# Short-convolution layer on one core: f's deep operand prepared later, and V' read ahead of d's split

## The chip, the cores and the metric

The kernel runs on one core of a Trainium2 chip. The metric is device time in microseconds (us). The kernel before takes 794.39 us, the median of three runs (793.05 to 795.4). Its engines are named as in the profile: PE (TensorE's matmuls; PEld its weight loads), DVE (VectorE), ACT (ScalarE), POOL (GpSimd) and SP (SyncE, which only issues transfers).

## The reference

One layer of a hybrid encoder; with the depth used here it is the short-convolution mixer in a sandwich norm. x is 1024 positions by 1024 channels in float32, and each branch is 2048 wide.

```python
def short_conv_mixer(u, w_in, conv_w, w_out):
    z, bg, cg, v = jnp.split(u @ w_in.astype(u.dtype), 4, axis=-1)
    y = bg * causal_dwconv(cg * v, conv_w) * jax.nn.silu(z)
    return y @ w_out.astype(u.dtype)

h = h + rms_norm(short_conv_mixer(rms_norm(h, pre), ...), post)
```

The input projection is 1024 x 1024 by 1024 x 8192, the convolution has three taps along the positions, and the output projection is 1024 x 2048 by 2048 x 1024.

## The kernel before, in words

**Precision.** Every operand of a matmul is split into a high part in fp32r and a low part, the rest. A product is done in three passes: low by high, high by low, high by high (L221 to L223, 128x128 by 128x512; L780 to L782, 128x128 by 128x256, in the smaller products). A split is an ACT instruction for the high part (a CAST) and a DVE subtraction for the low part. `split` (L160, L161), `split_high` and `split_low` (L168, L187) let DVE read the source from SBUF. `split_by_bank` (L181 to L183) has ACT copy the source into a PSUM bank, named beside, as well, and DVE reads it there; there is one such bank.

**Products.** The channels are worked in chunks c = p // 2 of two pairs p each: the even pair holds the columns CG and V, the odd pair Z and BG. The four block products of a pair are done as seven, a to g, with sums and differences of weight blocks (`add_s` on POOL, L148 to L156) and of the operand u (the tiles u_a to u_g, made once). A product of a pair is twelve 512-wide matmuls: wal, wah and so on are the low and high parts of its weight operand in the current pair, and px and pv are its banks in PSUM. From chunk DEEP = 3 on product b, and from chunk DEEP_F = 4 on product f, are replaced, for the two pairs of a chunk at once, by seven products of half the size. These are the slots written "bX'" and "fX'" below ("fc" is f's product c'); six 256-wide matmuls each, with weight operands dwb and dwf and the sums dsb and dsf behind them (`deep_sums`, L734 to L738, POOL).

**f's operand.** Product f of a chunk in seven needs u_f in another form. It is made once, in three steps:

- `deep_parts("f", [k])`: high and low part of quarter k of u_f are added on POOL into a page deepf (L701, 128x512). Four of them.
- `deep_subs("f", [k])`: four differences on POOL (L707 to L710, 128x256) on the quarters k and k + 2. Two calls, eight instructions.
- `deep_split("f", i)` for i = c', e', d', g': two halves each, ACT writes the high part ufXh (L160), DVE the low part ufXl (L161).

The same three steps make the operand of product b before, in pairs 4 to 6.

**Order.** PE's order is the list `slots`, built by hand. A tile framework gives each engine its instructions in the order in which the Python loop issues them, and each engine runs its queue in that order. After the matmuls of a slot the loop calls `prepare(n)`, which issues the splits of weights for all slots that start within LEAD = 7.0 us of the end of this one by a fixed clock (2.72 us for a product, 0.72 for a small one). Then comes the slot's own follow-up: `after(p, i)` (copies of a bank to SBUF on ACT, L229; additions and products on DVE and POOL), `deep_after` for b's small products (L787), `deep_after_f` for f's (L803 to L816). Then come transfers, weight sums, pieces of the output side, and last the entry of the table `UNDER`, if there is one for this slot. `UNDER` is what places the steps of the operands of b and f.

Around the change a chunk with f in seven goes like this on PE. Even pair: c, e, b a', b b', d, f a', f b', a of the next pair, b c', b e', g. Odd pair: c, f c', f e', e, b f', f f', b d', f d', d, b g', f g', a of the next pair, g. So the bank X' (px2f, from f c') and the bank V' (pv2f, from f e') are both finished around product e, and `deep_after_f` adds each to a half of the page snc on DVE (L814, 128x256). f f', later, adds onto V's bank again, so PE has to wait until L814 has read it.

In pairs 6 to 8, where f's operand is made, the last chunk without f in seven (c = 3) also ends with its convolution: gate (L271), first tap on ACT (L657), two more on DVE (L666), then the products with the gates and SiLU (L248 to L258, L1012, L1017), and the output y.

Of the kernel before, what the change touches and what calls it, by code (L numbers as in the profile page):

```python
# [17 lines left out]
DEEP_F = 4  # L18
# [5 lines left out]
def kernel(  # L24
# [48 lines left out]
    def page(name, dtype=F32, shape=(HB,)):  # L73

        return pages.tile([P, *shape], dtype, tag="pg", name=name, bufs=PAGES)
# [83 lines left out]
    def split(src, hi, lo):  # L159
        nc.scalar.copy(hi, src)  # L160
        nc.vector.tensor_sub(lo, src, hi.bitcast(F32))  # L161
# [8 lines left out]
    def by_seven(z, c):  # L170

        return c >= DEEP if z == "b" else DEEP_F <= c < NC - 1
# [524 lines left out]
    def deep_parts(z, ks):  # L697

        for k in ks:
            deep[z, k] = page(f"deep{z}{k}")  # L700
            nc.gpsimd.tensor_add(deep[z, k], UH[z][:, k].bitcast(F32), UL[z][:, k].bitcast(F32))  # L701

    def deep_subs(z, ks):

        for k in ks:
            (b11, b12), (b21, b22) = ((t[:, :HH], t[:, HH:]) for t in (deep[z, k], deep[z, k + KQ]))
            nc.gpsimd.tensor_sub(b12, b12, b11)  # L707
            nc.gpsimd.tensor_sub(b22, b22, b12)
            nc.gpsimd.tensor_sub(b11, b22, b11)
            nc.gpsimd.tensor_sub(b21, b21, b22)  # L710
# [3 lines left out]
    def deep_split(z, i):  # L714

        k0, l0 = DEEP_U[i]
        ls = slice(l0, l0 + HH)
        own = z == "f" or i != "e'"
        if own:
            deep[z, i] = [tmp.tile([P, KQ, HH], F32R, tag="ub", name=f"u{z}{i[0]}{h}_deep", bufs=14) for h in "hl"]  # L720
        for k in range(KQ):
            hi, lo = (t[:, k] for t in deep[z, i]) if own else (UH[z][:, k, ls], UL[z][:, k, ls])
            split(deep[z, k0 + k][:, ls], hi, lo)
# [212 lines left out]
    for p in range(2, len(PAIRS)):  # L936
# [29 lines left out]
        ("a", 2 * DEEP): lambda: (deep_split("b", "c'"), deep_split("b", "e'")),  # L966
        ("g", 2 * DEEP - 1): lambda: deep_split("b", "d'"),
        ("c", 2 * DEEP): lambda: deep_split("b", "g'"),
        ("d", 2 * DEEP_F - 3): lambda: deep_parts("f", [0]),
        ("f", 2 * DEEP_F - 3): lambda: deep_parts("f", [2]),  # L970
        ("d", 2 * DEEP_F - 2): lambda: deep_parts("f", [1]),
        ("f", 2 * DEEP_F - 2): lambda: deep_parts("f", [3]),
        ("g", 2 * DEEP_F - 2): lambda: deep_subs("f", [0]),
        ("c", 2 * DEEP_F - 1): lambda: deep_subs("f", [1]),
        ("e", 2 * DEEP_F - 1): lambda: deep_split("f", "c'"),
        ("d", 2 * DEEP_F - 1): lambda: deep_split("f", "e'"),
        ("f", 2 * DEEP_F - 1): lambda: deep_split("f", "d'"),
        ("g", 2 * DEEP_F - 1): lambda: deep_split("f", "g'"),
    }


# [7 lines left out]
    def prepare(n):  # L989
        while ready[0] < len(slots) and at[ready[0]] < at[n + 1] + LEAD:  # L990
            slot = slots[ready[0]]
            if slot[2:]:
                z, i, c = slot
                deep_prep(z, c, i)
            elif slot[::-1] not in wt:
                split_w(*slot[::-1])
            ready[0] += 1

    first_chunk("")
    for n, slot in enumerate(slots):  # L1000
        if slot[2:]:
            z, i, c = slot
            deep_product(z, c, i)
            prepare(n)
            if z == "f":
                deep_after_f(c, i)
                continue
            deep_after(c, i)
            if (i, c) == ("f'", NC - 1):
                third_unit(0)  # L1010
            elif i == "g'" and not by_seven("f", c):
                nc.scalar.activation(sn[2 * c + 1, "a"], sn[2 * c + 1, "a"], AF.Silu)  # L1012
            continue
        i, p = slot
        f7 = by_seven("f", p // 2)
        product(p, i)
        prepare(n)  # L1017
        after(p, i)
        q, prev = p + 1, p // 2 - 1
        if p == 2:  # L1020
            first_chunk(i)
        if i == "c":
            if p % 2 and p // 2 < DEEP:
                nc.scalar.activation(sn[p, "a"], sn[p, "a"], AF.Silu)
            if p % 2 == 0 and p in TODO:
                fetch_t(TODO[q])
            if p % 2 == 0 and p > 2:
                fetch_s(prev)
            if p % 2 == 0 and p in TODO:
                add_t(TODO[p], [0, 1])  # L1030
            if p % 2 == 0 and p // 2 >= DEEP:
                deep_sums("b", p // 2, 1)
        elif i == "e":
            add_s(q, "ecdf" if f7 else "ec")
            if f7 and p % 2 == 0:
                for part in (0, 1):
                    deep_sums("f", p // 2, part)
            if p % 2 and q in TODO:
                fetch_t(TODO[q])
            elif p in TODO and p % 2 == 0:  # L1040
                add_t(TODO[p], [2, 3])
        elif i == "d":
            if p + 2 <= END:
                fetch(p + 2)
            if not f7:
                add_s(q, "d")
            if p in TODO and p % 2 == 0:
                add_t(TODO[q], [0, 1])
            if p % 2 == 0 and p > 2:
                add_y(prev)  # L1050
        elif i == "f":
            add_s(q, "f")
            if p == 2:
                add_y(0)
        elif i == "g":
            if p % 2 and q <= END and q // 2 >= DEEP:
                deep_sums("b", q // 2, 0)
        elif i == "a":
            if prev >= 0 and p % 2 == 0 and by_seven("f", prev):
                for t in (sn[p - 1, "c"], sn[p - 1, "a"]):  # L1060
                    nc.scalar.activation(t, t, AF.Silu)
                nc.gpsimd.tensor_mul(cvs[prev][:, HB:], sn[p - 1, "c"], sn[p - 1, "e"])
            if p % 2 and p in TODO:
                add_t(TODO[p], [2, 3])
        if DEEP < NC and (i, p) in UNDER:
            UNDER[i, p]()
        if p == END - 1 and i in "cd":
            fetch_unit()
        if p == END:
            if i in "acg":  # L1070
                split_unit()
            elif i == "d":
                third_unit(2)
            if i in "ac":
                fetch_unit()
            elif i == "d":
                load_small("b", "B2")
            elif i == "f":
                load_small("b", "A1")
                load_small("b", "B1")  # L1080
                fetch_s(NC - 1)
            elif i == "g":
                for n in ("A2", "B3", "X"):
                    load_small("b", n)
                split_small("b", "B2")
                split_small("b", "B1")
                sums_y("b", "d", nc.vector)
                split_small("b", "A1")
# [238 lines left out]
```

## Time and profile before

| | before |
|---|---|
| median of three runs | 794.39 us |
| profiled execution | 794.88 us |
| its span | 793.1 us |
| PE busy | 773.6 us |
| DVE busy | 649.9 us |
| ACT busy | 420.1 us |
| POOL busy | 392.4 us |
| mean granted clock of TensorE | 0.993 |

The span is the time from the first to the last instruction that the profile shows; the profiled execution's own time is 1.8 us longer. A line of the timeline gives the start in us, the busy time in us, the engine, the source line, the operation, output<-inputs, the tile's shape, and how many instructions the line stands for. In brackets stands the idle time just before it, and the instruction whose end let it go. Matmuls overlap: a 512-wide one shows 0.39 us, but the next starts 0.23 us after it.

### The profile page before, as it was taken

The page shows a single profiled execution, that of the slowest core. Times are in us where ns is not written, and L with a number is a line of the kernel's source. Part 1 is how long each engine was busy: PE and PEld are TensorE (multiplying, and loading weights), DVE is VectorE, ACT ScalarE, POOL GpSimd, SP SyncE. Part 2 cuts the span into 40 slices and gives each one's busy share as a digit, 9 for nine tenths or more (in the row PEclk, how much of TensorE's full clock was granted, in tenths as well). Part 3 has the DMA queues.
Part 4 walks back from the last instruction along what each step waited for, and adds up shares of the span by engine and source line. Part 5 has one row for each costly group of instructions (what it writes and reads, how often), then busy time and mean ns, then how long its engine had stood idle before and what let it go on. Part 6 is the DMA issues. An engine that isn't in the chain of part 4 may idle for free. (4 is left out here: it accounts for less than half of the span.)

```text
span 793.1 us, 11970 instructions
## 1 busy us (share of the span) xinstructions
PE 773.6 (98%) x4050; PEld 664.7 (84%) x4050; DVE 649.9 (82%) x964; ACT 420.1 (53%) x775; POOL 392.4 (49%) x337
## 2 busy tenths in 40 slices
PE   8999999896999999999999999999999999999996
PEld 7888888785888888888888888888888889889985
DVE  6899657977587888888979798876779899986985
ACT  7655424335455556465554646464644565844821
POOL 2516579667364737384747474746555110630041
PEclk9999999998999999999999999999999999999999
DMA  9211431312327364453748383725243979885445
GB/s 318 55 54 31 116 108 38 94 53 79 119 95 219 120 193 155 158 185 127 239 127 259 107 271 110 256 82 158 74 127 107 346 250 351 306 260 190 130 159 186
DMA packets 115822, 127.18 MB, mean 160 GB/s; under 512 B 7416, under 2 KB 74032, under 8 KB 115760
## 3 DMA queue, kind: packets, MB, share of 16 engines
q1 hardware_dynamic: 115744, 126.41, 49.4%
q8 instruction: 32, 0.52, 0.3%
q14 instruction: 30, 0.25, 0.1%
q10 hardware_dynamic: 16, 0.00, 0.0%
HBM read 91.78 MB, written 34.60 MB: 159 GB/s over the span
## 5 line engine op out<-in xcount | busy, mean ns | idle before, releaser
L252 POOL TENSOR_TENSOR sne<-sne,cv 128x512 f32<-128x512 f32 x15 | 20.7, 1378 | 154.7 <-DVE cv L666 126.1
L182 ACT COPY beside<-raw 128x512 f32<-128x512 f32 x77 | 45.5, 590 | 31.6 <-DVE dwb1l L183 21.5
L221 PE MATMUL px<-u_c,wcl 128*128 128x512 f32 x124 | 49.2, 397 | 7.1 <-ACT sna L229 7.1
L229 ACT COPY sna<-px 128x512 f32<-128x512 f32 x30 | 17.6, 587 | 66.1 <-PE px L223 66.1
L152 POOL TENSOR_TENSOR se<-raw,raw 128x512 f32<-128x512 f32 x31 | 49.3, 1589 | 5.6 <-DMA raw<-in_sc_w_in 4.1
L666 DVE SCALAR_TENSOR_TENSOR cv<-gpad,cw,cv 128x1024 f32<-128x1024 f32 x32 | 42.2, 1319 | 11.4 <-ACT cv L657 11.2
L223 PE MATMUL px<-u_c,wch 128*128 128x512 f32 x124 | 49.0, 395 | 0.0
L222 PE MATMUL px<-u_c,wch 128*128 128x512 f32 x124 | 49.0, 395 | 0.0
L221 PE MATMUL px<-u_d,wdl 128*128 128x512 f32 x124 | 48.6, 392 | 0.0
L221 PE MATMUL px<-u_a,wal 128*128 128x512 f32 x124 | 48.6, 392 | 0.0
L222 PE MATMUL px<-u_a,wah 128*128 128x512 f32 x124 | 48.5, 391 | 0.0
L222 PE MATMUL px<-u_d,wdh 128*128 128x512 f32 x124 | 48.5, 391 | 0.0
L222 PE MATMUL px<-u_g,wgh 128*128 128x512 f32 x124 | 48.4, 391 | 0.0
L221 PE MATMUL px<-u_g,wgl 128*128 128x512 f32 x124 | 48.4, 390 | 0.0
L222 PE MATMUL pv<-u_e,weh 128*128 128x512 f32 x124 | 48.4, 390 | 0.0
L221 PE MATMUL pv<-u_e,wel 128*128 128x512 f32 x124 | 48.4, 390 | 0.0
L223 PE MATMUL px<-u_d,wdh 128*128 128x512 f32 x124 | 48.4, 390 | 0.0
L223 PE MATMUL px<-u_a,wah 128*128 128x512 f32 x124 | 48.3, 389 | 0.0
L223 PE MATMUL px<-u_g,wgh 128*128 128x512 f32 x124 | 48.3, 389 | 0.0
L223 PE MATMUL pv<-u_e,weh 128*128 128x512 f32 x124 | 48.2, 389 | 0.0
L154 POOL TENSOR_TENSOR sc<-se,raw 128x512 f32<-128x512 f32 x31 | 46.0, 1485 | 2.4
L148 POOL TENSOR_TENSOR raw<-raw,raw 128x512 f32<-128x512 f32 x31 | 46.2, 1491 | 0.0
(538 smaller groups left out, 2739.8 us busy)
## 6 DMA issues: line engine op xcount, KB each, us to landing
raw<-in_sc_w_in SPq DMA_DIRECT2D x128, 256.0 KB, 4.3
y_d<-cv SPq DMA_DIRECT2D x16, 512.0 KB, 3.3
s_d<-s SPq DMA_DIRECT2D x32, 256.0 KB, 3.5
t<-in_sc_w_out SPq DMA_DIRECT2D x32, 256.0 KB, 3.7
t_d<-t SPq DMA_DIRECT2D x32, 256.0 KB, 4.0
tb<-in_sc_w_out SPq DMA_DIRECT2D x16, 256.0 KB, 4.3
s<-y_d SPq DMA_DIRECT2D x16, 256.0 KB, 4.9
xr<-in_x SPq DMA_DIRECT2D x16, 256.0 KB, 3.8
```

Source lines behind the costliest of these rows:

```text
L148: nc.gpsimd.tensor_sub(t, block(p, 0, 0), t)
L152: nc.gpsimd.tensor_add(t, block(p, 1, 0), block(p, 1, 1))
L154: nc.gpsimd.tensor_sub(t, sums[p, "e"], block(p, 0, 0))
L182: nc.scalar.copy(b, src)
L221: nc.tensor.matmul(ps, lo, UH[i][:, k], start=first and k == 0, stop=False, skip_group_check=True)
L222: nc.tensor.matmul(ps, hi, UL[i][:, k], start=False, stop=False, skip_group_check=True)
L223: nc.tensor.matmul(ps, hi, UH[i][:, k], start=False, stop=last, skip_group_check=True)
L229: nc.scalar.copy(t, banks[p, "v" if i == "e" else "x"])
L252: nc.gpsimd.tensor_mul(t, t, cvs[c][:, HB:])
L666: nc.vector.scalar_tensor_tensor(cvs[c], gpad[:, j : j + L], tap(c, j), cvs[c], op0=ALU.mult, op1=ALU.add)
```

## The change

f's operand is prepared later. Its four sums (L701) stood behind d5, f5, d6 and f6; now two stand behind d6, one behind f6, one behind g6. Its differences stood behind g6 and c7; now behind e7 and d7. Its splits stood behind e7, d7, f7 and g7, in the last chunk with f whole; now behind c8, e8, d8 and a9, in the first chunk with f in seven, each ahead of the small product that reads it. The first small products that read them are f c', f e', f d' and f g' of chunk 4.

The loop also changes where it handles f c' and f e': the two reads L814 are issued before `prepare`, and after f c' `prepare` is left out, so that what it would have issued comes after f e'.

```diff
-        ("d", 2 * DEEP_F - 3): lambda: deep_parts("f", [0]),
-        ("f", 2 * DEEP_F - 3): lambda: deep_parts("f", [2]),
-        ("d", 2 * DEEP_F - 2): lambda: deep_parts("f", [1]),
-        ("f", 2 * DEEP_F - 2): lambda: deep_parts("f", [3]),
-        ("g", 2 * DEEP_F - 2): lambda: deep_subs("f", [0]),
-        ("c", 2 * DEEP_F - 1): lambda: deep_subs("f", [1]),
-        ("e", 2 * DEEP_F - 1): lambda: deep_split("f", "c'"),
-        ("d", 2 * DEEP_F - 1): lambda: deep_split("f", "e'"),
-        ("f", 2 * DEEP_F - 1): lambda: deep_split("f", "d'"),
-        ("g", 2 * DEEP_F - 1): lambda: deep_split("f", "g'"),
+        ("d", 2 * DEEP_F - 2): lambda: deep_parts("f", [0, 2]),
+        ("f", 2 * DEEP_F - 2): lambda: deep_parts("f", [1]),
+        ("g", 2 * DEEP_F - 2): lambda: deep_parts("f", [3]),
+        ("e", 2 * DEEP_F - 1): lambda: deep_subs("f", [0]),
+        ("d", 2 * DEEP_F - 1): lambda: deep_subs("f", [1]),
+        ("c", 2 * DEEP_F): lambda: deep_split("f", "c'"),
+        ("e", 2 * DEEP_F): lambda: deep_split("f", "e'"),
+        ("d", 2 * DEEP_F): lambda: deep_split("f", "d'"),
+        ("a", 2 * DEEP_F + 1): lambda: deep_split("f", "g'"),
...
             deep_product(z, c, i)
-            prepare(n)
+
+            early = (z, i) in (("f", "c'"), ("f", "e'"))
+            if early:
+                deep_after_f(c, i)
+            if (z, i) != ("f", "c'"):
+                prepare(n)
             if z == "f":
-                deep_after_f(c, i)
+                if not early:
+                    deep_after_f(c, i)
                 continue
```

PE's order is the same in both. On POOL, in pairs 5 and 6 of before (raw, se, sc and sf are weight sums, dsb b's sums of a chunk, cv, gpad the convolution's products, deepf the sums of u_f):

```order
L148 TENSOR_TENSOR raw_10_1056<-raw_00_1052,raw_10_1056 128x512
L701 TENSOR_TENSOR deepf_1223<-u_f 128x512
L258 TENSOR_TENSOR cv_1142<-snc_1166,sne_1190 128x512
L156 TENSOR_TENSOR sf_1244<-raw_01_1054,sc_1194 128x512
L701 TENSOR_TENSOR deepf_1246<-u_f 128x512
L734 TENSOR_TENSOR dsb_3_1300<-raw_01_1216 128x256
```

The same place on POOL in the changed kernel:

```order
L148 TENSOR_TENSOR raw_10_1056<-raw_00_1052,raw_10_1056 128x512
L258 TENSOR_TENSOR cv_1142<-snc_1166,sne_1190 128x512
L156 TENSOR_TENSOR sf_1242<-raw_01_1054,sc_1194 128x512
L734 TENSOR_TENSOR dsb_3_1296<-raw_01_1216 128x256
L735 TENSOR_TENSOR dsb_3_1296<-dsb_3_1296,raw_01_1054 128x256
L737 TENSOR_TENSOR dsb_3_1323<-raw_01_1054,raw_01_1216 128x256
L738 TENSOR_TENSOR dsb_3_1323<-raw_01_1054,dsb_3_1296 128x256
L152 TENSOR_TENSOR se_1351<-raw_10_1218,raw_11_1220 128x512
L154 TENSOR_TENSOR sc_1353<-se_1351,raw_00_1214 128x512
L148 TENSOR_TENSOR raw_10_1218<-raw_00_1214,raw_10_1218 128x512
L701 TENSOR_TENSOR deepf_1404<-u_f 128x512
L701 TENSOR_TENSOR deepf_1406<-u_f 128x512
```

Two of the sums have moved down behind the weight sums of a whole pair, and two stand one behind the other where one stood. On DVE, from the convolution of chunk 3 to the splits of pair 8, before (ufel and ufdl are low parts of f's operand, wgl, wcl and wel of weights of pair 8, sna and snc pages of pair 7):

```order
L666 SCALAR_TENSOR_TENSOR cv_1561<-gpad,cw,cv_1561 128x1024 x2
L187 TENSOR_TENSOR wgl_1578<-raw_11_1220,wgh_1577 128x512
L248 TENSOR_TENSOR sne_1528<-px_1432,sne_1528 128x512
L161 TENSOR_TENSOR ufel_deep<-deepf_1223,ufeh_deep 128x256
L161 TENSOR_TENSOR ufel_deep<-deepf_1408,ufeh_deep 128x256
L187 TENSOR_TENSOR wcl_1611<-sc_1532,wch_1610 128x512
L255 TENSOR_TENSOR snc_1506<-pv_1512,snc_1506 128x512
L161 TENSOR_TENSOR ufdl_deep<-deepf_1223,ufdh_deep 128x256
L161 TENSOR_TENSOR ufdl_deep<-deepf_1408,ufdh_deep 128x256
L787 TENSOR_TENSOR sna_1449<-px2b_1359,sna_1449 128x256
L187 TENSOR_TENSOR wel_1647<-se_1530,weh_1646 128x512
```

And in the changed kernel:

```order
L666 SCALAR_TENSOR_TENSOR cv_1551<-gpad,cw,cv_1551 128x1024 x2
L187 TENSOR_TENSOR wgl_1568<-raw_11_1220,wgh_1567 128x512
L248 TENSOR_TENSOR sne_1520<-px_1430,sne_1520 128x512
L187 TENSOR_TENSOR wcl_1599<-sc_1524,wch_1598 128x512
L255 TENSOR_TENSOR snc_1502<-pv_1504,snc_1502 128x512
L787 TENSOR_TENSOR sna_1447<-px2b_1355,sna_1447 128x256
L187 TENSOR_TENSOR wel_1629<-se_1522,weh_1628 128x512
```

The four halves are gone from this stretch, as are ufcl's two a little ahead of it; the eight low parts of f's operand stand from product c8 on, the last two directly ahead of L787 and wel of pair 9. On DVE in a steady chunk (here chunk 5: dwf2l and wdl weights, snc the page that L814 adds to, dwb b's operand), before:

```order
L183 TENSOR_TENSOR dwf2l_2288<-beside,dwf2h_2287 128x512
L183 TENSOR_TENSOR wdl_2301<-beside,wdh_2300 128x512
L814 TENSOR_TENSOR snc_2092<-px2f_2196,snc_2092 128x256
L814 TENSOR_TENSOR snc_2292<-pv2f_2306,snc_2292 128x256
L161 TENSOR_TENSOR dwb_5_2327<-raw_01_2005,dwb_5_2327 128x256
```

And in the changed kernel:

```order
L183 TENSOR_TENSOR dwf2l_2288<-beside,dwf2h_2287 128x512
L814 TENSOR_TENSOR snc_2092<-px2f_2196,snc_2092 128x256
L814 TENSOR_TENSOR snc_2292<-pv2f_2301,snc_2292 128x256
L183 TENSOR_TENSOR wdl_2310<-beside,wdh_2309 128x512
L161 TENSOR_TENSOR dwb_5_2327<-raw_01_2005,dwb_5_2327 128x256
```

The two reads and wdl have changed places.

## The prediction

> **What bounds the kernel now.** I read the page's head first, then the waits of PE, then PE's timeline around each wait, then the queue of the engine that was named, and back from there to what that engine had been doing.
>
> ```profile
> span 793.1 us, 11970 instructions
> PE 773.6 (98%) x4050; PEld 664.7 (84%) x4050; DVE 649.9 (82%) x964; ACT 420.1 (53%) x775; POOL 392.4 (49%) x337
> PE px L221 <- ACT sna L229: 7.1, 1, 7.1
> PE pv L221 <- DVE wfl L187: 2.3, 1, 2.3
> PE pv2f L780 <- DVE snc L814: 1.9, 6, 0.4
> ```
>
> TensorE is busy for 98% of the span, so only its pauses can be won. The three lines of waits (total us, count, longest) are all there is behind the start-up: one wait of 7.1, one of 2.3, and six of about 0.3. All three lie where the change works: wfl and sna in pairs 6 to 8, L814 in every later chunk. The timeline gives what each pause really costs, by the distance between two starts against the same distance undisturbed.
>
> ```profile
> 147.10 0.39 PE L223 MATMUL px<-u_d,wdh 128*128 128x512 f32 x1
> 149.80 0.55 PE L221 MATMUL pv<-u_f,wfl 128*128 128x512 f32 x1 [2.32 <-DVE wfl L187]
> 154.21 0.39 PE L221 MATMUL px<-u_a,wal 128*128 128x512 f32 x1
> 163.83 0.39 PE L221 MATMUL pv<-u_e,wel 128*128 128x512 f32 x1
> 166.55 0.28 PE L780 MATMUL pv2b<-u_b,dwb2l 128*128 128x256 f32 x1
> 179.42 0.39 PE L223 MATMUL px<-u_g,wgh 128*128 128x512 f32 x1
> 186.89 0.79 PE L221 MATMUL px<-u_c,wcl 128*128 128x512 f32 x1 [7.08 <-ACT sna L229]
> 191.64 0.40 PE L221 MATMUL pv<-u_e,wel 128*128 128x512 f32 x1
> 211.03 0.39 PE L221 MATMUL pv<-u_e,wel 128*128 128x512 f32 x1
> 248.33 0.39 PE L221 MATMUL pv<-u_e,wel 128*128 128x512 f32 x1
> 440.52 0.39 PE L780 MATMUL pv2f<-u_f,dwf2l 128*128 128x256 f32 x1 [0.36 <-DVE snc L814]
> 550.16 0.39 PE L221 MATMUL pv<-u_e,wel 128*128 128x512 f32 x1
> ```
>
> A product is 12 matmuls: from e7's first (163.83) to the next product's first (166.55) are 2.72, or 0.227 a step. **Stall 1**: from d6's last matmul (147.10) to a7's first (154.21) lie 7.11, where one step and f6's twelve need 13 x 0.227 = 2.95. Lost: 4.16, though the wait is only 2.32. **Stall 2**: from g7's last (179.42) to e8's first (191.64) lie 12.22, again 13 steps; lost: 9.27, with a wait of 7.08. **V' waits**: from e9 (211.03) to e11 (248.33) is one undisturbed chunk, 37.30. From e11 to e27 (550.16) are eight chunks, 301.83 against 298.40; lost: 3.43, in the six waits on L814 and the slow first step behind each.
>
> What a pause costs beyond its own length is the clock. The windows view (length, then busy us of PE, PEld, DVE, ACT and POOL, then PE's granted clock) shows it behind stall 1 and behind a wait on L814:
>
> ```profile
> 149.80:153.50 3.70, 3.70 (x9) 2.91 (x10) 3.60 (x7) 1.14 (x2) 1.34 (x1) 0.54 0.46 127
> 440.50:446.00 5.50, 5.48 (x35) 4.98 (x36) 4.68 (x11) 3.18 (x6) 0.00 (x0) 1.00 0.72 206
> ```
>
> After 2.3 us of idleness the clock is 0.54, after 0.36 it stays 1.00: the point lies between. The Trainium skill, "TensorE: Matmul & The Clock Gate", section "What's actually happening", puts the drop after about 3.4 us without work, and recovery after about 3.4 us of work. The 2.3 us of this trace do not agree. By the page's threshold stall 1 would be worth 2.3, and the sum below would come out 1.8 later; the measured 4.16 decides.
>
> **Stall 1, part by part.** First VectorE's queue up to wfl and wal, then GpSimd's sums L701 of f's operand:
>
> ```profile
> 145.05 2.94 DVE L161 TENSOR_TENSOR ubdl_deep<-deepb,ubdh_deep 128x256 fp32r<-128x256 f32 x2
> 147.91 1.75 DVE L187 TENSOR_TENSOR wfl<-sf,wfh 128x512 fp32r<-128x512 f32 x1
> 149.58 1.84 DVE L161 TENSOR_TENSOR ubgl_deep<-deepb,ubgh_deep 128x256 fp32r<-128x256 f32 x2
> 151.34 0.68 DVE L187 TENSOR_TENSOR wal<-raw,wah 128x512 fp32r<-128x512 f32 x1
> 134.64 1.75 POOL L701 TENSOR_TENSOR deepf<-u_f 128x512 f32<-128x512 f32 x1
> 139.23 1.47 POOL L701 TENSOR_TENSOR deepf<-u_f 128x512 f32<-128x512 f32 x1
> 149.74 1.40 POOL L701 TENSOR_TENSOR deepf<-u_f 128x512 f32<-128x512 f32 x1 [0.63 <-DVE wfl L187]
> ```
>
> wfl took 1.75 where wal of the same shape, with GpSimd idle, took 0.68: the two engines work by turns when both read SBUF. wfl ended at 149.66, and PE wanted it at 147.33. The change takes two sums (134.64 and 139.23) out of GpSimd's queue ahead of it. Each is one turn of VectorE's, about 1.2 (1.75 less 0.55, the part of a contended step in which VectorE itself works): wfl then ends near 147.25, and stall 1 goes. If only one turn comes through, wfl ends at 148.46 and 1.1 stay. Bounds of the gain 3.0 to 4.16; I take 4.16, because the sums are whole instructions of the same queue.
>
> The same sums now stand right behind wfl, two where one stood. ubgl's two halves (1.84 beside one sum) get a second sum against them, about 1.0 more, and wal 0.6: wal ends near 147.25 + 1.84 + 1.0 + 0.6 = 150.7, where PE wants it at 154.21 - 4.16 = 150.05. **New wait at a7: 0.7**, between 0 and 1.2 (the sum runs beside PSUM readers only, or holds wfl up as well).
>
> **Stall 2.** f's splits in pair 7 on VectorE, and what ScalarE did behind them:
>
> ```profile
> 167.67 2.12 DVE L161 TENSOR_TENSOR ufcl_deep<-deepf,ufch_deep 128x256 fp32r<-128x256 f32 x2 [1.71 <-ACT ufch_deep L160]
> 176.60 1.85 DVE L161 TENSOR_TENSOR ufel_deep<-deepf,ufeh_deep 128x256 fp32r<-128x256 f32 x2
> 181.74 2.75 DVE L161 TENSOR_TENSOR ufdl_deep<-deepf,ufdh_deep 128x256 fp32r<-128x256 f32 x2 [0.99 <-ACT ufdh_deep L160]
> 185.21 0.63 ACT L1012 ACTIVATE sna<-sna 128x512 f32<-128x512 f32 x1 [3.20 <-DVE sna L787]
> 186.26 0.58 ACT L229 COPY sna<-px 128x512 f32<-128x512 f32 x1
> 192.03 2.40 DVE L161 TENSOR_TENSOR ufgl_deep<-deepf,ufgh_deep 128x256 fp32r<-128x256 f32 x2
> ```
>
> c8 waits for the copy of a8's bank (186.26), which stands in ScalarE's queue behind the SiLU of sna (185.21), which waited 3.20 for VectorE's L787; and that stands behind ufdl, in a queue that ufcl and ufel had already made late. Taken out of that stretch: 2.12 + 1.71 idle ahead of it, 1.85, 2.75 + 0.99, so 9.4 before the copy, and PE's wait is 7.08. With wfl's 2.33 gained as well, the copy that ended at 186.84 ends near 175.1, and PE is through with g7 at 179.42 + 0.23 - 4.16 + 0.7 = 176.2: **stall 2 goes whole, 9.27**, with 1.1 to spare. What is late next there is the copy itself: should ScalarE lose more than 1.1, that excess comes back as a wait.
>
> **The first chunk with f in seven (pairs 8 and 9)** gets what was taken away: four splits, of which ufgl stood there already. By the rows above 2.12 + 1.85 + 2.75 = 6.72 are new on VectorE, all ahead of wel of pair 9:
>
> ```profile
> 176.77 1.41 POOL L252 TENSOR_TENSOR sne<-sne,cv 128x512 f32<-128x512 f32 x1 [5.82 <-DVE sne L248]
> 164.26 0.74 POOL L710 TENSOR_TENSOR deepf<-deepf 128x256 f32<-128x256 f32 x1
> 191.52 1.74 POOL L156 TENSOR_TENSOR sf<-raw,sc 128x512 f32<-128x512 f32 x1
> 204.08 0.90 DVE L187 TENSOR_TENSOR wel<-se,weh 128x512 fp32r<-128x512 f32 x1
> ```
>
> wel ended at 204.98, 6.05 ahead of e9 (211.03). By that alone 0.7 are missing. GpSimd adds to it: eight differences of 0.74 come about a pair later, and four of them (3.0) stand between L252 and the sums that dwf1l and wel need. L252 (176.77) comes earlier by wfl's 2.33 and ufcl's 2.12, at 172.3; from there to sf's end (193.26) were 16.5, with 3.0 more 19.5, and half of the differences that dwf1l reads cost 1.5: 193.3. Idle time of before that lay in the 16.5 may take some of that off. Then come dwf1h and dwf1l (1.3), ufgl (0.8 to 2.4) and wel (0.9 to 1.5): wel ends between 196.3 and 198.5 by that, or sooner, and e9 is wanted at 211.03 - 13.43 + 0.7 = 198.3, so GpSimd's side ends 0.2 late at worst. With both, and GpSimd's own instructions stretched by the contention (sf took 1.74 here), I take 1.0 at e9, and 0.6 more for d8 and c9, whose operands come from the same queues. **New waits 1.6**, bounds 0 and 2.7.
>
> **The reads of V'.** In one steady chunk on VectorE, beside the end of wel and e21 on PE:
>
> ```profile
> 434.55 1.45 DVE L187 TENSOR_TENSOR wel<-se,weh 128x512 fp32r<-128x512 f32 x1
> 439.11 0.69 DVE L183 TENSOR_TENSOR wdl<-beside,wdh 128x512 fp32r<-128x512 f32 x1 [0.83 <-ACT beside L182]
> 440.05 0.42 DVE L814 TENSOR_TENSOR snc<-pv2f,snc 128x256 f32<-128x256 f32 x1
> 436.54 0.39 PE L221 MATMUL pv<-u_e,wel 128*128 128x512 f32 x1
> ```
>
> VectorE idles 0.83 ahead of wdl, waiting for ScalarE's copy. Both L814 (2 x 0.42) fit into just that hole, so the read of V' ends near 439.1 and not at 440.47, and the wait of 0.36 goes in every chunk. Behind the moved reads stands wdl, which is no later than before. But PE then catches up with the next thing: wel ended at 436.00, 0.54 ahead of e21. Each wait costs 3.43 / 6 = 0.57, so after one gain wel is the end that binds. If VectorE and ScalarE keep their pace, the gain up to chunk 12 is 0.6, and the last wait's 0.57 comes whole: 1.2. If they follow, it is 3.43. I take **1.5**, near the lower end, since the copies on which VectorE waited 0.83 aren't moved.
>
> **Sum**, on the profiled execution's 794.88: - 4.16 - 9.27 + 0.7 + 1.6 - 1.5 = 782.25. The median shown, 794.39, lies 0.49 below that execution: 781.8.
>
> **The rivals.** *A, everything comes through*: no new wait and the whole 3.43: 794.39 - 13.43 - 3.43 = 777.5. For it: VectorE was busy 82%, so there is room somewhere. Against it: wel's 0.54. Chance 0.2. *B, the new waits fall together and pull the clock*: a7 at 1.2, the first chunk at 2.7 and, as e9 then waits near 2 us, a spell at half clock that costs what stall 1's did beyond its wait, 4.16 - 2.32 = 1.8; V' at 1.2. That gives 794.39 - 13.43 + 1.2 + 2.7 + 1.8 - 1.2 = 785.5. For it: 2.3 us were enough at 149.80. Against: no single wait above 1.2 in my count. Chance 0.18. *C, slower*: in the first chunk each half of the eight lows waits out a GpSimd instruction. Eight at 1.45 (as wel had it, 434.55) are 11.6; the differences and sums of GpSimd's queue, stretched likewise, put 3.9 on top; a clock spell 1.8, and a7 1.2. From 13.43 + 1.2 = 14.6 on it is slower; these 18.5 give 798.3. For it: wfl's 1.75 against wal's 0.68. Against: ufgl's two halves took 2.40 in that very chunk, not 2.9, and 6.05 were to spare. Chance 0.04. The Trainium skill, "SBUF — State Buffer", section "SBUF: two separate sides", speaks for C: it calls the port pair of VectorE and GpSimd an exclusive lock, held for the whole instruction, the loser blocking fully. The trace agrees as far as wfl's 1.75 goes. *D, the stalls only move*: c8 still waits on ScalarE's queue, behind other work, and no time is won within 2.4 us: 794.4. Chance 0.03.
>
> **Numbers.** The forecast itself has 0.55, from 780 to 784. With A and B the range is 777.5 to 786.5; outside it lie C, D and the corners of the unknown costs. About 0.3%, or 2.4 us, can be told from no change. Faster 0.93 (forecast, A, B), same 0.03, slower 0.04.
>
> **What would show it.** In the changed profile: no wait of PE on wfl and none of over 1 us on sna; a7's first matmul some 0.7 late on wal; e9's on wel by about 1; no clock under 0.9 after the start; no wait on L814, and waits on wel or wcl in chunks 9 to 12 in its place. It is wrong if c8 still waits for ScalarE, if a clock spell appears in pairs 8 to 10, or if the chunks 9 to 12 go at 37.30 each.

## The result, and the profile after

The changed kernel takes 782.39 us (median of 6 runs, 782.01 to 782.59), against 794.12 for the kernel before on the same chip (6 runs, 793.05 to 795.53). The ratio is 0.9849, with a 95% interval from 0.9837 to 0.9862. 781.8 had been forecast, with a range of 777.5 to 786.5. Its profiled execution took 782.01 us. The page's head and the waits of PE (us in total, times, longest) after:

```profile
span 780.2 us, 11978 instructions
PE 769.1 (99%) x4050; PEld 660.5 (85%) x4050; DVE 647.9 (83%) x964; ACT 419.0 (54%) x775; POOL 393.3 (50%) x337
PE pv L221 <- DVE wel L187: 0.8, 1, 0.8
PE px L221 <- DVE wcl L187: 0.6, 2, 0.3
PE px L221 <- DVE wal L187: 0.4, 1, 0.4
```

The three groups of waits of before are gone: none on wfl, none on sna, none on L814. In their place stand three small ones, and they are those that the prediction named: wal of pair 7, wel of pair 9, and wcl in the late chunks. PE's timeline after, at the points that were used before (d6's last matmul, f6, a7, g7's last, e8, e9, e11, e27):

```profile
146.99 0.39 PE L223 MATMUL px<-u_d,wdh 128*128 128x512 f32 x1
147.40 0.47 PE L221 MATMUL pv<-u_f,wfl 128*128 128x512 f32 x1
150.77 0.50 PE L221 MATMUL px<-u_a,wal 128*128 128x512 f32 x1 [0.41 <-DVE wal L187]
176.07 0.39 PE L223 MATMUL px<-u_g,wgh 128*128 128x512 f32 x1
179.01 0.39 PE L221 MATMUL pv<-u_e,wel 128*128 128x512 f32 x1
199.82 0.47 PE L221 MATMUL pv<-u_e,wel 128*128 128x512 f32 x1 [0.81 <-DVE wel L187]
237.21 0.39 PE L221 MATMUL pv<-u_e,wel 128*128 128x512 f32 x1
537.26 0.39 PE L221 MATMUL pv<-u_e,wel 128*128 128x512 f32 x1
```

From d6's last matmul to a7 are 3.78 us now, where 2.95 is undisturbed: of stall 1, 0.83 is left, 0.18 of it at f6 and 0.65 at a7. From g7's last to e8 are 2.94: nothing of stall 2 is left. From e8 to e9 are 20.81, where the same stretch took 211.03 - 191.64 = 19.39 before: 1.42 are new, 0.96 of them at e9 itself and the rest at d8 and c9. From e9 to e11 are 37.39, and from e11 to e27 300.05, against 37.30 and 301.83: 0.09 lost and 1.78 won. Together - 3.33 - 9.27 + 1.42 + 0.09 - 1.78 = - 12.87; the spans differ by 12.9. Two readings rest on other engines: the copy of a8's bank on ScalarE, and wel of pair 9 on VectorE.

```profile
174.84 0.58 ACT L229 COPY sna<-px 128x512 f32<-128x512 f32 x1
...
195.59 2.39 DVE L161 TENSOR_TENSOR ufgl_deep<-deepf,ufgh_deep 128x256 fp32r<-128x256 f32 x2
198.24 1.44 DVE L187 TENSOR_TENSOR wel<-se,weh 128x512 fp32r<-128x512 f32 x1
```

The copy ends at 175.42, 0.9 before PE is through with g7 (176.07 + 0.23). wel, behind ufgl, ends at 199.68, and e9 starts at 199.82.

### The profile page after: what moved, and what is told of

The parts are those of the page before. It is cut to its first block, busy times and chain, and to the rows that moved or that the text cites. A ratio compares the mean times of both kernels' runs of the same rounds, so it can differ in the third digit from the quotient of the medians.

```text
span 780.2 us, 11978 instructions
## 1 busy us (share of the span) xinstructions
PE 769.1 (99%) x4050; PEld 660.5 (85%) x4050; DVE 647.9 (83%) x964; ACT 419.0 (54%) x775; POOL 393.3 (50%) x337
## 5 line engine op out<-in xcount | busy, mean ns | idle before, releaser
L156 POOL TENSOR_TENSOR sf<-raw,sc 128x512 f32<-128x512 f32 x31 | 47.1, 1519 | 0.0
L148 POOL TENSOR_TENSOR raw<-raw,raw 128x512 f32<-128x512 f32 x31 | 46.7, 1508 | 0.0
```

What stands on the lines that cost most here:

```text
L148: nc.gpsimd.tensor_sub(t, block(p, 0, 0), t)
L156: nc.gpsimd.tensor_sub(t, block(p, 0, 1), sums[p, "c"])
```

## The experiments

Times are medians; each ratio is to the kernel before on the same chip, with its 95% interval. The profiled executions' spans are used only where a trace is read.

### One half of the change at a time

The table alone is the changed kernel with these lines as they were before:

```diff
             deep_product(z, c, i)
-
-            early = (z, i) in (("f", "c'"), ("f", "e'"))
-            if early:
-                deep_after_f(c, i)
-            if (z, i) != ("f", "c'"):
-                prepare(n)
+            prepare(n)
             if z == "f":
-                if not early:
-                    deep_after_f(c, i)
+                deep_after_f(c, i)
```

> The table of the change with the loop of before: f's operand later, the reads of V' in their old place. Theory (the stretches are separate): the changed kernel's trace gives the chunks from e11 to e27 300.05 us against 301.83 before, so the reads are worth 1.8, and this kernel takes 782.4 + 1.8 = 784.2 us, with the six waits of PE on L814 back, about 0.3 each. Rival (the reads are worth the whole 3.4 that the waits cost, and the waits on wcl came from elsewhere): 785.8. Rival (the reads are worth nothing, since wcl and wel would have bound the chunks in any case): 782.4.

Measured: 784.95 us, ratio 0.9877 (0.9864 to 0.9890). That lies between the theory and its first rival, and the waits of PE say why:

```profile
PE pv2f L780 <- DVE snc L814: 2.6, 7, 0.7
```

There are seven waits, not six: in chunk 4, where wel of pair 9 is late, the reads in their old place come late too (0.7; from e9 to e11 are 38.33 here and 37.39 in the changed kernel, so 0.94 with the slow steps behind it). From e11 to e27 this kernel takes 540.41 - 238.49 = 301.92 by its trace, 1.87 more than the changed one. 1.87 + 0.94 = 2.81 against 2.56 between the two medians. So the new place of the reads is worth 1.8 us in the steady chunks, as forecast, and most of one more us in the first chunk, which the forecast had not seen: there the two halves of the change help each other.

The reads alone are the kernel before with those lines as the change has them.

> The table of before with the loop of the change: only the reads of V' stand earlier. Theory: both stalls stay as they were (13.4 us), the six waits on L814 go, and waits on wcl or wel take the place of half of them: 794.1 - 1.8 = 792.3 us. Rival (all of the 3.4 comes through when the stalls are there): 790.7.

Measured: 793.58 us, ratio 0.9979 (0.9970 to 0.9989), 1.7 us less than the kernel before. The waits on L814 are gone, three on wcl of 0.3 stand in chunks 10 to 12, and e11 to e27 take 546.97 - 246.61 = 300.36. The theory holds: the gain is 0.9 to 2.4 us by the interval, and the rival's 3.4 lies outside it. Single executions spread from 791.7 to 794.7; the last section takes this up.

### One part of the table at a time

The sums without the splits (differences and splits stand where they stood before; the reads stand as in the change):

```diff
-        ("g", 2 * DEEP_F - 2): lambda: deep_parts("f", [3]),
-        ("e", 2 * DEEP_F - 1): lambda: deep_subs("f", [0]),
-        ("d", 2 * DEEP_F - 1): lambda: deep_subs("f", [1]),
-        ("c", 2 * DEEP_F): lambda: deep_split("f", "c'"),
-        ("e", 2 * DEEP_F): lambda: deep_split("f", "e'"),
-        ("d", 2 * DEEP_F): lambda: deep_split("f", "d'"),
-        ("a", 2 * DEEP_F + 1): lambda: deep_split("f", "g'"),
+        ("g", 2 * DEEP_F - 2): lambda: (deep_parts("f", [3]), deep_subs("f", [0])),
+        ("c", 2 * DEEP_F - 1): lambda: deep_subs("f", [1]),
+        ("e", 2 * DEEP_F - 1): lambda: deep_split("f", "c'"),
+        ("d", 2 * DEEP_F - 1): lambda: deep_split("f", "e'"),
+        ("f", 2 * DEEP_F - 1): lambda: deep_split("f", "d'"),
+        ("g", 2 * DEEP_F - 1): lambda: deep_split("f", "g'"),
```

> The loop of the change and its places for the four sums of u_f (behind d6, f6, g6), but differences and splits where they stood before. Theory (the stalls are one chain): stall 1 goes, but the splits of pair 7 hang on GpSimd's differences, which come no earlier (its queue gets two sums more in pair 6), so the copy of a8's bank ends near 187 as before, PE reaches c8 some 3.3 us sooner and waits there for 10 us or more instead of 7.1: 792 to 793 us, of which 1.8 under the kernel before are the reads of V'. Rival (the stalls are separate, and each is won by its own part): 794.1 - 4.16 + 0.8 - 1.8 = 789.0.

Measured: 792.11 us, ratio 0.9969 (0.9957 to 0.9981). The waits of PE:

```profile
PE px L221 <- ACT sna L229: 6.8, 1, 6.8
PE px L221 <- DVE sne L248: 1.7, 1, 1.7
PE px L221 <- DVE wcl L187: 0.9, 3, 0.3
```

Stall 1 is gone, and e7 starts at 160.81 by this trace, against 162.28 in the run with the reads alone, where stall 1 is there. But c8 starts at 185.62 here and at 185.41 there: what PE gains at f6 it waits away at g7 and c8, 8.5 in place of 7.1. Of the 2.5 us that this kernel wins by its ratio, 1.7 are the reads. GpSimd's last difference starts at 168.01 here and at 167.34 in the kernel before, so the splits in pair 7 could come no sooner. The theory holds, with the one long wait split in two.

The splits without the sums (sums and differences stand where they stood before; the reads stand as in the change):

```diff
-        ("d", 2 * DEEP_F - 2): lambda: deep_parts("f", [0, 2]),
-        ("f", 2 * DEEP_F - 2): lambda: deep_parts("f", [1]),
-        ("g", 2 * DEEP_F - 2): lambda: deep_parts("f", [3]),
-        ("e", 2 * DEEP_F - 1): lambda: deep_subs("f", [0]),
-        ("d", 2 * DEEP_F - 1): lambda: deep_subs("f", [1]),
+        ("d", 2 * DEEP_F - 3): lambda: deep_parts("f", [0]),
+        ("f", 2 * DEEP_F - 3): lambda: deep_parts("f", [2]),
+        ("d", 2 * DEEP_F - 2): lambda: deep_parts("f", [1]),
+        ("f", 2 * DEEP_F - 2): lambda: deep_parts("f", [3]),
+        ("g", 2 * DEEP_F - 2): lambda: deep_subs("f", [0]),
+        ("c", 2 * DEEP_F - 1): lambda: deep_subs("f", [1]),
```

> The loop of the change and its places for the four splits (behind c8, e8, d8, a9), but sums and differences where they stood before. Theory (stall 2 hangs on the splits alone, and stall 1 on the sums alone): stall 1 stays with its 2.3 us wait and the half clock (4.16), stall 2 goes, and since PE comes to the first chunk 3.3 us later than in the changed kernel, while the differences no longer stand in GpSimd's queue there, no wait on wel of pair 9 is left: 794.1 - 9.27 - 1.8 = 783.0, up to 783.6. So the splits alone would give all but 1 us of the change. Rival (the splits only help together with the sums, since the copy of a8's bank needs wfl's 2.3 us too): c8 still waits, 785 us or more.

Measured: 782.76 us, ratio 0.9854 (0.9840 to 0.9868), within 0.4 us of the whole change, and stall 1 still stands in it:

```profile
PE pv L221 <- DVE wfl L187: 2.3, 1, 2.3
PE px L221 <- DVE wcl L187: 0.8, 3, 0.3
```

No wait on wal or wel is left. e8 starts at 180.91 here and at 179.01 in the changed kernel, e9 at 200.28 and 199.82: of 1.9 us that the sums' move had won by e8, 0.46 are left at e9. Against the run with the reads alone, which differs from this one only in the splits, the spans are 789.9 and 780.8: the splits are worth 9.1, and e8 to e9 take 19.37 here, with no new wait. So the splits' move carries the change, and the two sums' move pays for its own new waits and little more. One part of the expectation did not come: the half clock behind stall 1 is not in this trace, and the stall costs 5.54 - 2.95 = 2.59 in it, not 4.16. One of the four executions took 784.39, at a mean granted clock of 0.995 against 0.998 to 0.999 in the three others (782.6 to 782.8); it may be one in which the clock fell, but no trace shows that.

### What makes wfl late

The prediction took each sum ahead of wfl for one turn of VectorE's, 1.2 us. Putting one of the two back tests that price:

```diff
-        ("d", 2 * DEEP_F - 2): lambda: deep_parts("f", [0, 2]),
+        ("d", 2 * DEEP_F - 3): lambda: deep_parts("f", [0]),
+        ("d", 2 * DEEP_F - 2): lambda: deep_parts("f", [2]),
```

> The changed kernel with one of the two moved sums put back behind d5, ahead of wfl of pair 6. Theory (each 512-wide sum in GpSimd's queue costs VectorE one turn of about 1.2 us): wfl ends near 148.45 instead of 147.25, f6 waits about 1.0; a7's wait of 0.4 goes, since one sum less stands against ubgl: 782.4 + 1.0 - 0.7 = 782.7 us, and the granted clock stays at 1.00 behind a wait of 1.0. Rival (stall 1 came from both sums together, the first of them in time that GpSimd had to spare): no wait at f6, 781.7. Rival (1.0 us of idleness can halve the clock): 784 in some executions.

Measured: 785.67 us (785.62 to 785.79 in four runs), ratio 0.9879 (0.9862 to 0.9895). None of the three had it: the wait at f6 is the whole 2.31 again. VectorE and GpSimd in that run's timeline:

```profile
145.15 2.94 DVE L161 TENSOR_TENSOR ubdl_deep<-deepb,ubdh_deep 128x256 fp32r<-128x256 f32 x2
148.02 1.75 DVE L187 TENSOR_TENSOR wfl<-sf,wfh 128x512 fp32r<-128x512 f32 x1
...
146.35 1.46 POOL L148 TENSOR_TENSOR raw<-raw,raw 128x512 f32<-128x512 f32 x1
147.78 1.44 POOL L701 TENSOR_TENSOR deepf<-u_f 128x512 f32<-128x512 f32 x1
```

And the same place in the changed kernel:

```profile
143.70 2.95 DVE L161 TENSOR_TENSOR ubdl_deep<-deepb,ubdh_deep 128x256 fp32r<-128x256 f32 x2
146.57 0.68 DVE L187 TENSOR_TENSOR wfl<-sf,wfh 128x512 fp32r<-128x512 f32 x1
...
144.89 1.48 POOL L148 TENSOR_TENSOR raw<-raw,raw 128x512 f32<-128x512 f32 x1
146.73 3.10 POOL L701 TENSOR_TENSOR deepf<-u_f 128x512 f32<-128x512 f32 x2 [0.36 <-DVE ubdl_deep L161]
```

With one sum back, GpSimd goes from L148 straight on to L701, which is running when wfl starts, and wfl takes 1.75. In the changed kernel GpSimd stands still for 0.36 us at just that moment, because its first sum waits for ubdl; wfl starts first (146.57 against 146.73) and takes 0.68. So 1.75 - 0.68 = 1.07 of the 2.4 us by which wfl ended earlier are that pause, and not a turn saved. A second run keeps one sum early and gives GpSimd a pause at wfl:

```diff
-        ("d", 2 * DEEP_F - 2): lambda: deep_parts("f", [0, 2]),
-        ("f", 2 * DEEP_F - 2): lambda: deep_parts("f", [1]),
+        ("d", 2 * DEEP_F - 3): lambda: deep_parts("f", [0]),
+        ("f", 2 * DEEP_F - 2): lambda: deep_parts("f", [2, 1]),
```

> As the run with one sum behind d5, but the second sum stands behind f6 instead of d6, so that GpSimd has nothing to do when VectorE comes to wfl of pair 6; the same number of sums ahead of wfl as in that run. Theory (not the number of sums makes wfl late, but whether GpSimd has an instruction running beside it): ubdl's second half still ends near 148.0, wfl then takes 0.7 instead of 1.75 and ends near 148.7, f6 waits about 1.1 instead of 2.3, a7 does not wait: 782.4 + 1.1 - 0.7 = 782.8 us. Rival (each sum is one turn, whatever stands beside wfl): the wait stays at 2.3 and the time at 785.7. On the clock: if 1.1 us of idleness are enough to halve it, 784 to 785 with slow steps of 0.43 behind f6.

Measured: 783.26 us, ratio 0.9858 (0.9842 to 0.9873). The wait at f6 and VectorE there:

```profile
148.98 0.47 PE L221 MATMUL pv<-u_f,wfl 128*128 128x512 f32 x1 [1.26 <-DVE wfl L187]
...
145.29 2.94 DVE L161 TENSOR_TENSOR ubdl_deep<-deepb,ubdh_deep 128x256 fp32r<-128x256 f32 x2
148.16 0.68 DVE L187 TENSOR_TENSOR wfl<-sf,wfh 128x512 fp32r<-128x512 f32 x1
148.76 0.74 DVE L161 TENSOR_TENSOR ubgl_deep<-deepb,ubgh_deep 128x256 fp32r<-128x256 f32 x2
```

wfl takes 0.68 and ubgl 0.74, no wait at a7 is left, and the clock stays. The theory holds: with the same sum ahead, wfl takes 1.75 when an instruction of GpSimd is running as it starts, and 0.68 when none is, and the wait at f6 falls from 2.31 to 1.26. But the number of sums ahead counts too, for the 1.26 that are left: ubdl, just ahead of wfl, starts as late in these two runs as before the change, and 1.24 earlier in the changed kernel, each measured from d6's last matmul. VectorE a little further ahead, before, with one sum back, and in the changed kernel (u_b is b's operand):

```profile
138.04 2.95 DVE L161 TENSOR_TENSOR u_b<-deepb,u_b 128x256 fp32r<-128x256 f32 x2
143.91 1.22 DVE L265 TENSOR_TENSOR cv<-cv,sna 128x512 f32<-128x512 f32 x1
...
138.13 2.40 DVE L161 TENSOR_TENSOR u_b<-deepb,u_b 128x256 fp32r<-128x256 f32 x2
143.46 1.77 DVE L265 TENSOR_TENSOR cv<-cv,sna 128x512 f32<-128x512 f32 x1
...
137.93 1.84 DVE L161 TENSOR_TENSOR u_b<-deepb,u_b 128x256 fp32r<-128x256 f32 x2
142.70 1.07 DVE L265 TENSOR_TENSOR cv<-cv,sna 128x512 f32<-128x512 f32 x1
```

One sum fewer gains 0.55 at u_b and loses it again at L265, where a weight sum of GpSimd's now meets it; two fewer gain 1.11 and 0.15.

### The new waits

The split for g' once more later:

```diff
-        ("a", 2 * DEEP_F + 1): lambda: deep_split("f", "g'"),
+        ("e", 2 * DEEP_F + 1): lambda: deep_split("f", "g'"),
```

> The changed kernel with only the split for g' moved once more, from behind a9 to behind e9 (its reader, f g', comes after d9). Theory (VectorE's queue makes wel of pair 9 late, ufgl's 2.39 us directly ahead of it): wel ends some 2.3 us sooner, e9's wait of 0.8 (1.0 with the slow step behind it) goes, nothing else changes: 781.4 us. Rival (GpSimd's sums bind, and ufgl only fills the time): the wait stays, 782.4. Rival (ufgl, now behind the reads of V', pushes dwb or gpad late and f f' or b g' wait): 782.4 or more.

Measured: 781.58 us, ratio 0.9827 (0.9813 to 0.9842). wel of pair 9 ends 2.01 ahead of e9 by this trace, where it ended 0.14 ahead, and the wait is gone. The theory holds.

The sums one by one:

```diff
-        ("d", 2 * DEEP_F - 2): lambda: deep_parts("f", [0, 2]),
-        ("f", 2 * DEEP_F - 2): lambda: deep_parts("f", [1]),
-        ("g", 2 * DEEP_F - 2): lambda: deep_parts("f", [3]),
+        ("d", 2 * DEEP_F - 2): lambda: deep_parts("f", [0]),
+        ("f", 2 * DEEP_F - 2): lambda: deep_parts("f", [2]),
+        ("g", 2 * DEEP_F - 2): lambda: deep_parts("f", [1]),
+        ("c", 2 * DEEP_F - 1): lambda: deep_parts("f", [3]),
```

> The changed kernel with the four sums one by one: behind d6, f6, g6 and c7, so that only one stands against ubgl's two halves. Theory (the second sum costs wal of pair 7 one turn, and the chain to e9 starts from PE's e7, so that it comes sooner too): a7 loses its 0.6 to 0.75, and all behind moves with it: 781.7 us. Rival (the chain to e9 hangs on VectorE and GpSimd alone): a7's wait goes and e9's grows by as much, 782.4.

Measured: 782.36 us, ratio 0.9837 (0.9822 to 0.9852): no gain. The wait at a7 is gone, but the rival was right only in the sum. Of the 0.65, some 0.2 went at d8 (a wait of 0.17 on a copy of ScalarE's, which was not there before), and e9's wait kept its size. The rest was given back in chunk 11: three waits on wcl instead of two, e11 to e27 in 537.53 - 237.12 = 300.41.

### What sets the pace of chunks 9 to 12

One VectorE instruction less ahead of wcl, with the sum L303 left out:

```diff
             nc.vector.tensor_add(t1, t1, cv[:, HB:])
-            nc.vector.tensor_sub(t0, t1, t0)
             nc.vector.tensor_sub(t2, cv[:, :HB], t0)
```

> The changed kernel without the second of the three sums of y (L303) in the chunks from 9 on: this leaves out part of the computation, one VectorE instruction of 0.7 us in each of these chunks, which stands ahead of wcl. Theory (VectorE's queue sets the pace of chunks 9 to 12, 37.85 us against PE's 37.30): the waits on wcl go, chunks e11 to e27 take 298.4 us, 1.65 less: 780.7. Rival (ScalarE's copies through the one bank beside set the pace): the loop stays at 37.85 and so do the waits: 782.4.

Measured: 780.77 us, ratio 0.9818 (0.9803 to 0.9832). No wait on wcl is left, and e11 to e27 take 536.21 - 237.75 = 298.46, PE's own time. VectorE's queue sets the pace there; ScalarE's copies do not.

The same three sums on GpSimd:

```diff
-            nc.vector.tensor_add(t1, t1, cv[:, HB:])
-            nc.vector.tensor_sub(t0, t1, t0)
-            nc.vector.tensor_sub(t2, cv[:, :HB], t0)
+            nc.gpsimd.tensor_add(t1, t1, cv[:, HB:])
+            nc.gpsimd.tensor_sub(t0, t1, t0)
+            nc.gpsimd.tensor_sub(t2, cv[:, :HB], t0)
```

> The changed kernel with the three sums of y (L302 to L304, chunks 9 to 12) on GpSimd instead of VectorE, at the same place of the program; nothing is left out. Theory (VectorE's queue sets the pace there, and GpSimd stands idle for 4.6 us just then): VectorE gets 2.0 us less to do ahead of wcl, gives back some 0.7 for each of its instructions that now meets one of GpSimd's, and still no wait on wcl or wel is left: 780.7 us. Rival (GpSimd's three sums, 1.3 to 1.7 each, make wcl, dwf1l and wel work by turns and its own next sums late): 782.4 or slower.

Measured: 787.54 us, ratio 0.9911 (0.9897 to 0.9925): 5 us slower than the changed kernel, 4.2 of them between e11 and e27 (541.69 - 237.45 = 304.24 against 300.05). The rival was right, and by more than it had said. VectorE and GpSimd at the sums of chunk 11:

```profile
456.17 1.56 DVE L332 TENSOR_TENSOR tb<-tb 128x256 f32<-128x256 f32 x1
457.83 1.34 DVE L335 TENSOR_TENSOR t<-tb,tb 128x256 f32<-128x256 f32 x1
459.09 0.41 DVE L814 TENSOR_TENSOR snc<-px2f,snc 128x256 f32<-128x256 f32 x1
459.43 1.44 DVE L187 TENSOR_TENSOR wcl<-sc,wch 128x512 fp32r<-128x512 f32 x1
...
456.16 1.30 POOL L302 TENSOR_TENSOR s<-s,cv 128x512 f32<-128x512 f32 x1
457.53 1.35 POOL L303 TENSOR_TENSOR s<-s,s 128x512 f32<-128x512 f32 x1
458.96 1.35 POOL L304 TENSOR_TENSOR s<-cv,s 128x512 f32<-128x512 f32 x1
```

L332, L335 and wcl, each beside one of the three, take 1.56, 1.34 and 1.44; in the changed kernel they take 0.41, 0.43 and 0.68. So VectorE saves 3 x 0.69 us and pays 2.8, and each wait on wcl grows to 1.0.

All moves at once, with the sums of u_f spread, both sets of differences behind e7, the split for g' behind e9, and the sums of y on GpSimd (the lines that the diffs above do not show):

```diff
-        ("e", 2 * DEEP_F - 1): lambda: deep_subs("f", [0]),
-        ("d", 2 * DEEP_F - 1): lambda: deep_subs("f", [1]),
+        ("e", 2 * DEEP_F - 1): lambda: deep_subs("f", [0, 1]),
```

> All that the runs pointed to, on the changed kernel, nothing left out: the four sums one by one behind d6, f6, g6 and c7; both sets of differences behind e7, where GpSimd idled 4.3 us; the split for g' behind e9; the three sums of y on GpSimd. Theory (the remaining waits are separate once VectorE no longer bounds chunks 9 to 12): 782.4 - 0.7 (a7) - 0.8 (e9) - 0.5 (c9, d8) - 1.65 (wcl, wel) = 778.8 us. Rival (what is gained ahead of chunk 9 is given back there, as in the run with the sums spread): 780 to 781.

Measured: 785.91 us, ratio 0.9891 (0.9877 to 0.9905). The first part came: no wait is left at a7, c9 and e9, and from e8 to e9 PE needs 198.52 - 179.15 = 19.37. A wait of 0.20 at c8, on ScalarE's copy, takes 0.5 of it back (e8 starts 3.44 after g7's last matmul, where it was 2.94). The sums of y took the rest back and more, with four waits on wcl of up to 1.0.

The last run keeps the first part and puts the sums of y half a chunk later, where VectorE mostly reads PSUM (against the run before it; the parameter that names the engine is left out):

```diff
         elif i == "e":
             add_s(q, "ecdf" if f7 else "ec")
+            if p % 2 and prev >= CH:
+                add_y(prev, nc.gpsimd)
...
-            if p % 2 == 0 and p > 2:
+            if p % 2 == 0 and p > 2 and prev < CH:
                 add_y(prev)
```

> The changed kernel with the sums of u_f, the differences and the split for g' placed as in the run with all moves, and the three sums of y of chunks 9 to 12 (from chunk 8's y on) on GpSimd, but half a chunk later, behind the weight sums that follow product e of the odd pair, where GpSimd idles 8.8 us (428.9 to 437.6 in the changed kernel's trace) and VectorE reads PSUM almost only; nothing is left out. Theory (the same 2.0 us of VectorE's work cost nothing where no instruction of VectorE with two SBUF sources stands beside them): the waits on a7, c9, e9 go (1.4, as in the run with all moves), and those on wcl and wel too (1.65): 782.4 - 3.05 = 779.3 us. Rival (the page of the convolution is released too late for the next first tap, L657, and VectorE waits for it): the loop stays above 37.5 us a chunk, 781 or more.

Measured: 779.78 us, ratio 0.9805 (0.9792 to 0.9818), the fastest of all. The same three sums on GpSimd in chunk 10 of this run, and L816, the VectorE instruction with two SBUF sources near them; then L816 and the last of the sums in chunk 9, and the load of g's weights that comes late there:

```profile
426.06 1.48 POOL L302 TENSOR_TENSOR s<-s,cv 128x512 f32<-128x512 f32 x1
427.62 1.30 POOL L303 TENSOR_TENSOR s<-s,s 128x512 f32<-128x512 f32 x1
429.00 1.37 POOL L304 TENSOR_TENSOR s<-cv,s 128x512 f32<-128x512 f32 x1
...
428.79 0.43 DVE L816 TENSOR_TENSOR gpad<-snc,sne 128x256 f32<-128x256 f32 x1
...
390.89 1.30 POOL L304 TENSOR_TENSOR s<-cv,s 128x512 f32<-128x512 f32 x1
391.14 1.33 DVE L816 TENSOR_TENSOR gpad<-snc,sne 128x256 f32<-128x256 f32 x1
...
397.83 0.19 PEld L221 LDWEIGHTS px<-u_g,wgl 128*128 128x128 f32 x1 [0.46 <-DVE sne L248]
```

No wait on wcl or wel is left, and wcl and wel end 1.6 to 3.0 ahead in chunks 9 to 12. e11 to e27 take 535.07 - 235.90 = 299.17. The forecast was 779.3; the 0.5 that is missing lies within the 0.77 by which this stretch exceeds PE's own 298.40. Some 0.66 of that are two late starts of product g, in chunks 9 and 11, each on VectorE's L248. In just these two chunks L816 meets one of the sums and takes 1.33 and 1.38; in chunks 10 and 12 it slips past them in 0.43 and 0.45, and g is not late. So the new place is nearly free, not wholly.

## Why the prediction was right, and where its steps were not

**Stall 2: right, and the main thing.** It was to go whole, 9.27, by the splits; it did, and the splits with the reads give all but 0.4 us of the change. The copy of a8's bank was to end near 175.1, 1.1 ahead of PE; it ended at 175.42, 0.9 ahead.

**Stall 1: the sum right, the step wrong.** wfl was to end near 147.25 and did (146.57 + 0.68). But "each is one turn of VectorE's, about 1.2" was wrong: with one sum back the wait is the whole 2.31, not 1.0. Both sums together were worth one such turn, 1.24, and a pause of GpSimd's, which waited for ubdl just then, was worth 1.07. That the end came out to the hundredth is luck. Nor does any row show the 0.55 from which the turn was worked out: alone wfl takes 0.68, so that meeting GpSimd costs it 1.07. The new wait at a7 was forecast as 0.7 and is 0.65.

**The first chunk: right.** 1.6 were forecast, 1.42 came, and e9 had about 1.0 of them as foretold. ufgl is what stood in the way, as moving it alone showed.

**V': right.** 1.5 were forecast, 1.78 came, with wcl as the next to be late where the prediction had worked out wel; it had left the sign of it open ("waits on wel or wcl"). That VectorE keeps its pace was the ground for the low end, and leaving one instruction out confirmed it.

**What the sum hid.** The terms were added as if each stood for itself. They do not. The sums without the splits would have brought next to nothing (792.1 with the reads, which make up most of that gain), since the splits of pair 7, on which the copy of a8's bank waits, then come no sooner; and together with the splits most of their gain is lost again by e9. The sum came out because the change has all three parts. And stall 1's 4.16 is a term of one execution: in the run with the splits the same wait costs 2.59, so 1.57 of the 4.16 are the slow clock, which the same pause brings in some traces and not in others. The prediction's reading that the clock falls somewhere between a pause of 0.36 and one of 2.3 does not hold as a fixed point.

**The rivals.** A (everything comes through) had the new waits against it, which are there. B had the right waits, but they stayed under 1 us each, and the clock at 1.00. C was a true mechanism in the wrong place: VectorE and GpSimd working by turns did cost more than it saved in the two runs with the sums of y on GpSimd in their old place; in the first chunk it did not. (The 3.9 that C put down to GpSimd's queue was worked out from no row.) D is out: c8 waits for nothing in the changed kernel.

## What to carry to other kernels

A step that is moved off one queue should be laid beside instructions that cannot meet it: with the same three sums on GpSimd the kernel took 785.9 us where VectorE reads two SBUF tiles beside them, and 779.8 where it mostly reads PSUM. Before gains of several stalls are added up, it pays to follow the later stall's chain back past the earlier one: if it hangs on something else, the earlier stall is only moved into it. And a stall's worth is read from the stretch it ends in (the next fixed point of PE), not from its wait.

## What the runs showed of the hardware

**The clock behind a pause of 2.3 us falls or stays.** In the traces of four kernels f6 waits for wfl equally long, 2.31 to 2.32 us. The clock behind it (windows view, columns as in the prediction), first with one sum early, then with the splits alone:

```profile
151.00:154.00 3.00, 3.00 (x9) 2.34 (x8) 2.90 (x7) 0.00 (x0) 0.00 (x0) 0.51 0.18 50
```

```profile
151.00:154.00 3.00, 3.00 (x15) 2.47 (x14) 2.90 (x6) 0.32 (x1) 0.25 (x1) 1.00 0.18 50
```

In the first the steps are fast up to 151.21, 1.3 us after the pause, and then slow for 3 us; in the kernel before they were slow from 149.80 on. In the second, and in the run with the reads alone, none is slow, and a7 follows 2.8 us after f6's start and not 4.4. This may be part of why executions of the kernel before lie between 792.7 and 795.9, and those with the reads alone between 791.7 and 794.7: a fall costs 1.57 us, and the profiled execution of the latter, without one, is the fastest of its twelve. That is argued and not shown, since each kernel has one trace. Nor is the fall a matter of chance alone: with one sum early all four executions lie within 785.6 to 785.8. Behind 1.26 us of idleness the trace shows no slow step, and four executions lie within 783.0 to 783.4. The Trainium skill, "TensorE: Matmul & The Clock Gate", section "What's actually happening", says that the window in which activity is watched is free-running and does not reset when a kernel starts; that the same pause falls out both ways agrees with it. Its idle window of about 3.4 us does not agree with a clock that falls after 2.3.

**VectorE's price for meeting GpSimd depends on GpSimd's instruction.** A 128x256 operation of VectorE with two SBUF sources takes 0.41 to 0.43 alone, and 1.34 and 1.56 beside the 128x512 sums of GpSimd's in the run with the sums of y; a 128x512 one takes 0.68 alone, and 1.44 (wcl) and 1.75 (wfl) beside them. The small one thus loses as much as the large one. Beside a 128x256 sum of GpSimd's a 128x512 one takes less, 1.22 (wdl in the run with one sum early). L814, whose one source is in PSUM, keeps its 0.41 beside L304. In the Trainium skill, "SBUF — State Buffer", section "SBUF: two separate sides", whichever of the two starts first holds the ports that they share for its whole instruction, and the other is blocked. These rows agree with it, and so does wfl in the changed kernel, which keeps its 0.68 although a sum starts 0.16 after it.
